# Expert stages: the gate-times-up product traced ahead of the scattered sums and unpinned, low parts of the rows on VectorE, the routing weights' copies behind the first gather

## The chip, the cores and the metric

The kernel runs on one core of one Trainium2 chip. The metric is device time in microseconds (us) of one launch. Before the change it is 1609.78 us, the median of three runs (1607.67 to 1613.72).

## The reference, cut to what matters

Two transformer blocks of two layers each run one after the other on 256 tokens of width 1024, in float32. The change touches only the mixture of experts of the first block, which is run once in each of its two layers:

```python
def grouped_moe(h, router_w, router_b, w_gate, w_up, w_down):
    t = h.reshape(B_ * S, D)
    scores = jax.nn.sigmoid((t @ router_w).astype(jnp.float32))
    sel = scores + router_b.astype(jnp.float32)
    ...  # best group of 4 experts, then the top 2 experts inside that group
    combine = jnp.einsum('nk,nke->ne', top_w, jax.nn.one_hot(top_idx, N_EXPERTS))
    for e in range(N_EXPERTS):
        he = jax.nn.silu(t @ w_gate[e]) * (t @ w_up[e])
        y = y + combine[:, e:e + 1] * (he @ w_down[e])
```

There are 16 experts with hidden width 512, so each layer reads 16 x 3 weight matrices of 2 MB, about 100 MB.

## The kernel before, in words

**An expert stage.** `moe(l)` first finds out which token goes to which expert and then runs eight pairs of experts, p = 0 to 7, two experts side by side on the two halves of TensorE's columns. The head, up to the first pair, goes like this. The 256 rows, as two halves t = 0 and 1, are normalised to `xn` (line 515, VectorE) and copied to DRAM as `xd` (line 1280, a DMA of GpSimd's queue). `parts(t)` splits the rows into a high part `xh` (a copy on ScalarE, line 1272) and a low part `xl`, which is the row less its high part (a subtraction on GpSimd, line 1273), both in an order of columns that reads every fourth element of `xn`. TensorE makes the router's logits, `scored` and a sigmoid make the scores `sc` (lines 1264 and 1288). A chain of small VectorE instructions from `sel` (line 1291) to `pick` (line 1317) chooses the experts; `rk` is a token's place within its expert, `cnt` and `cnti` (lines 1333 to 1338) are the numbers of tokens of the busiest expert of each pair, and `cs` (line 1346) are the routing weights, which `split` copies into a high part `ch` (ScalarE, line 203) and a low part `cl` (VectorE, line 204).

**The first gather.** For pair 0, `hot` builds one-hot tables `kept` on VectorE (line 1359), `gather` multiplies `xh` and `xl` with them on TensorE (line 1373, sixteen products for each half of the width) and ScalarE brings the results to `hg` (line 1377), the moving rows of the gate and up products. The tile of `hg` takes the place of `xn`, so its first write waits until `xn` has been read by the low parts and by the copy to DRAM. `tokens_of` builds further one-hot tables `ohb` on VectorE (line 1391, twelve instructions) from which the token numbers of the later pairs are made; those pairs fetch their rows with indirect DMAs.

**One pair.** `up(p)` runs the gate products `pg` and the up products `pu` (line 1479, 32 matrix instructions each in the trace), then calls `self.pending(2)`, then makes `hd` = silu(gate) on ScalarE (line 1489) and `hd` times up on VectorE (line 1490), then turns `hd` on TensorE (`turn_hidden`, line 184, tile `hT`), calls `self.pending(2)` again, turns the next pair's rows (`hgT`), and `down(p)` runs the down products `po` (line 1527). `self.pending` is the tail of the pair before: its four scattered sums, each two products on TensorE (`py`, lines 1514 and 1515) and an addition into `x` on VectorE (line 1517). Pairs 5 and 6 have a skipped block `rest` (branch at line 1614) between the up products and the sums.

**What sets the order.** The program is written through a planner: it places each engine's instructions by when they are ready in its own model and by program order. `keep_in_program_order`, here `pin`, holds an instruction behind the one that was traced just before it on its engine. So the pinned product of line 1490 stands behind the two additions of line 1517 of the first `pending(2)`. Numbers that branches need (`cnti`) are read into registers by `values_load` (lines 1612 and 1665); the planner has put these reads on TensorE's queue between the first gather and the first gate product. Weights are loaded by SyncE's queue (line 222) into 17 slots of 1 MB; a pair takes 12, and a slot's next load waits until the products that read it are done.

Of the kernel before, what the change touches and what calls it, by code (L numbers as in the profile page):

```python
# [11 lines left out]
F32 = mybir.dt.float32  # L12
# [3 lines left out]
AF = mybir.ActivationFunctionType  # L16
ALU = mybir.AluOpType
# [4 lines left out]
P = 128  # L22
# [98 lines left out]
class Net:  # L121
# [1107 lines left out]
    def moe(self, l):  # L1229
        nc, I, tc = self.nc, self.I, self.tc  # L1230
        V = nc.vector
        mm = nc.tensor.matmul
        A, B = self.scale_shift(l, 1)
        with self.phase(f"moe{l}", MOE_RING, True) as mp:
# [3 lines left out]
            pin = tc.keep_in_program_order  # L1238
# [24 lines left out]
                mm(pl, lg[t], self.fold, start=True, stop=True)  # L1263
                V.scalar_tensor_tensor(sc[:, t, :], pl, rs[t], rb, op0=ALU.mult, op1=ALU.add)

            def parts(t):
                for c in range(2):
                    sl = (slice(None), t, slice(512 * c, 512 * c + 512))

                    hi, lo = (e[sl].rearrange("p (k q) -> p k q", k=4) for e in (xh, xl))  # L1270
                    src = xn[sl].rearrange("p (q k) -> p k q", k=4)
                    pin(nc.scalar.copy(hi, src))
                    pin(nc.gpsimd.tensor_tensor(lo, src, hi.bitcast(F32), op=ALU.subtract))

            xd = self.dram.tile([S, D + NE], F32, name="xd")
            for t in range(2):
# [1 line left out]
                    self.norm_cols(self.norm_turn(self.x, t, k0), hT, t, k0)  # L1278
                rs[t] = self.norm_rows(self.x, t, xn, t)
                pin(nc.gpsimd.dma_start(xd[128 * t:128 * t + 128, 0:D], xn[:, t, :]))  # L1280
            parts(0)
            for t in range(2):
                logits(t)
                self.warm(WARM[t])
# [1 line left out]
                scored(t)  # L1286
            self.warm(WARM[2])
            nc.scalar.activation(sc, sc, AF.Sigmoid)
            parts(1)
            sel = mp.tile([P, 2, 16], F32, name="sel")  # L1290
            V.tensor_tensor(sel, sc, rbias.unsqueeze(1).to_broadcast([P, 2, 16]), op=ALU.add)

# [48 lines left out]
            cs = mp.tile([P, 2, 16], F32, name="cs")  # L1341
# [4 lines left out]
            V.tensor_tensor(cs, cs, den.unsqueeze(2).to_broadcast([P, 2, 16]), op=ALU.mult)  # L1346
            ch = mp.tile([P, 2, 16], F32R, name="ch")
            cl = mp.tile([P, 2, 16], F32R, name="cl")
            self.split(cs, ch, cl)
            nc.gpsimd.dma_start(xd[:, D:].rearrange("(t p) e -> p t e", p=P), cs)  # L1350

            def hot(ps, c0, n):

                m, ohs = 2 * len(ps), []
                io = slots[:, c0:c0 + n].unsqueeze(1).to_broadcast([P, m, n])
                for t in range(2):
                    oh = kept[:, t, :].rearrange("p (e s) -> p e s", e=m)
                    e = rk[:, t, 2 * ps[0]:2 * ps[0] + m].unsqueeze(2).to_broadcast([P, m, n])
                    V.tensor_tensor(oh, e, io, op=ALU.is_equal)
                    ohs.append(oh.rearrange("p e s -> p (e s)"))  # L1360
                return ohs
# [3 lines left out]
            def gather(k0, k1):  # L1365

                if not hg:
                    hg.append(self.sp.tile([P, 2, KD, P], F32, tag="xn", name="hg", bufs=1))
                for b0 in range(k0, k1, 2):
                    ph = self.bank([P, 2, 256], name="ph")  # L1370
                    for b in range(2):
                        for i, (t, xx) in enumerate(((0, xh), (0, xl), (1, xh), (1, xl))):
                            pin(mm(ph[:, b, :], xx[:, t, 128 * (b0 + b):128 * (b0 + b) + 128], oneh[t],
                                   start=i == 0, stop=i == 3))
                    for b in range(2):
                        k = b0 + b
                        nc.scalar.activation(hg[0][:, :, k, :], ph[:, b, :].rearrange("p (a c) -> p a c", a=2), AF.Identity,
                                             scale=self.ab[:, 0, k // 4, k % 4:k % 4 + 1],
                                             bias=self.ab[:, 1, k // 4, k % 4:k % 4 + 1])
# [5 lines left out]
            def tokens_of():  # L1385
                for h in range(2):
                    for t in range(2):
                        o = self.sp.tile([P, 3, 256], BF16, tag=("e2", "gt")[h], name="ohb")
                        e = rk[:, t, 4 + 6 * h:10 + 6 * h].rearrange("p (q j) -> p q j", j=2).unsqueeze(3)
                        for c, n, s0 in ((0, 64, 0), (128, 32, 64), (192, 32, 64)):  # L1390
                            V.tensor_tensor(o[:, :, c:c + 2 * n].rearrange("p q (j s) -> p q j s", j=2),
                                            e.to_broadcast([P, 3, 2, n]),
                                            slots[:, s0:s0 + n].unsqueeze(1).unsqueeze(1).to_broadcast([P, 3, 2, n]),
                                            op=ALU.is_equal)
                        ones_of.append(o)

            def indices():
                px = self.bank([P, 14], name="px")
                for p in range(2, 8):
                    h, q = (p - 2) // 3, (p - 2) % 3  # L1400
                    for c, col in ((0, p), (128, 6 + p)):
                        for t in range(2):
                            mm(px[:, col:col + 1], ones_of[2 * h + t][:, q, c:c + 128], self.tok[:, t:t + 1],
                               start=t == 0, stop=t == 1)

                none = mp.tile([P, 14], F32, name="none")
                V.tensor_copy(number[:, 2:], px[:, 2:])
                V.tensor_scalar(none[:, 2:], number[:, 2:], 0.5, 2.0 * S, op0=ALU.is_lt, op1=ALU.mult)
                V.scalar_tensor_tensor(idx[:, 2:], number[:, 2:], -1.0, none[:, 2:], op0=ALU.add, op1=ALU.add)
                for n in ("xh", "xl"):  # L1410
                    got.append(mp.tile([P, 2, D + NE], F32, tag=n, name=n))
                    V.memset(got[-1][:, :, D:], 0.0)
                rows(0, 2)
                rows(0, 3)
                rows(1, 2)

            def rows(i, p):

                nc.gpsimd.indirect_dma_start(got[i][:, p % 2, :], None, xd[:, :],
                                             bass.IndirectOffsetOnAxis(ap=idx[:, 6 * i + p:6 * i + p + 1], axis=0),  # L1420
                                             bounds_check=S - 1, oob_is_err=False)
# [43 lines left out]
            def up(p, W, between=None):  # L1465

                if p == 0:
                    oneh.extend(hot((0, 1), 0, 64))
                    gather(0, 4)
                    tokens_of()  # L1470
                q = slice(128 * (p % 2), 128 * (p % 2) + 128)
                pg = self.bank([P, 512], name="pg")
                pu = self.bank([P, 512], name="pu")
                for w, pp in ((W[0], pg), (W[1], pu)):
                    for k in range(KD):
                        if p == 0 and w is W[0] and k == 4:
                            gather(4, 8)
                        for j in range(2):
                            pin(mm(pp[64 * j:64 * j + 64, :], hg[0][:, p % 2, k, 64 * j:64 * j + 64], w[j][k // 4][:, k % 4, :],  # L1479
                                   start=k == 0, stop=k == KD - 1, tile_position=(0, 64 * j)))  # L1480
                if between:
                    between()
                if p == 0:
                    indices()

                if self.pending:
                    self.pending(2)
                hd = self.sp.tile([P, 512], F32, tag="e1", name="hd")
                pin(nc.scalar.activation(hd, pg, AF.Silu))
                pin(V.tensor_tensor(hd, hd, pu, op=ALU.mult))  # L1490
                hidT = self.sp.tile([P, 4, P], F32, tag="e2", name="hidT")
                turn_hidden(hd, hidT)
                if self.pending:
                    self.pending(2)
                Sm, ws = places([oneh[t][:, q] for t in range(2)], p) if p < FIRST else own_places.pop(0)
                if 1 <= p < 7:
                    columns(got[0][:, (p + 1) % 2, 0:D], P, hg[0][:, (p + 1) % 2])
                    own_places.append(known(p + 1, 0, kept[:, p % 2, :]))
                    if p < 6:
                        rows(1, p + 2)  # L1500
                    if p < 5:
                        rows(0, p + 3)
                return hidT, Sm, ws

            def turn_hidden(hd, out, bank=None):
                pt = bank.rearrange("p (k n) -> p k n", k=4) if bank is not None else self.bank([P, 4, P], name="hT")
                src = hd.rearrange("p (b q k) -> p b k q", b=2, k=2)
                for k in range(4):
                    self.tr(pt[:, k, :], src[:, k // 2, k % 2, :])
                V.tensor_copy(out, pt)  # L1510
# [951 lines left out]
```

## Time and profile before

| | |
|---|---|
| median of the runs | 1609.78 us (1607.67 to 1613.72) |
| the profiled execution: its time / its span | 1617.59 us / 1615.8 us |
| mean granted TensorE clock | 0.973 of full |
| busy share of the span: TensorE, VectorE, ScalarE, GpSimd | 92%, 57%, 42%, 9% |
| expert stage of layer 0, first gate product to last down product | 226.6 to 469.7 us |
| expert stage of layer 1, likewise | 640.9 to 865.5 us |
| HBM traffic | 422 MB read, 263 GB/s over the span |

All times in the rows are microseconds from the span's start unless marked ns. PE is TensorE's products, PEld its weight loads, DVE VectorE, ACT ScalarE, POOL GpSimd, SP SyncE; a "q" behind a name is the engine's sequencer. A timeline row gives the start, the duration (of all of a merged run, with its count), and in brackets the idle time of the engine before it with what ended it.

### The profile page before, as it was taken

How to read it: one execution, taken by the hardware profiler on the slowest of the kernel's cores; microseconds unless marked ns; L12 is line 12 of the kernel's file. 1: busy time of each engine (PE TensorE's matmuls, PEld its weight loads, DVE VectorE, ACT ScalarE, POOL GpSimd, SP SyncE). 2: the span in 40 equal slices, each digit the busy share in tenths (PEclk: the TensorE clock that was granted, in tenths of full speed). 3: DMA queues.
4: the chain of work that ended last, by engine and by line, in shares of the span. 5: the costliest groups of instructions: out<-in, count | busy, mean ns of one | idle time of the engine just before them, and what ended most of it. 6: DMA issues, size and time to landing. Idle time of an engine off the chain costs nothing. (4 is left out here: it accounts for less than half of the span.)

```text
span 1615.8 us, 22948 instructions
## 1 busy us (share of the span) xinstructions
PE 1494.5 (92%) x8719; PEld 1055.0 (65%) x8719; DVE 920.7 (57%) x1780; ACT 673.9 (42%) x1404; POOL 152.6 (9%) x200
## 2 busy tenths in 40 slices
PE   6999979888989996999888899999999999999998
PEld 3666633333349974443435787878888897788886
DVE  3765533232349985132325776766666776866665
ACT  3434421111135553111114355665555756665554
POOL 0320111000000002110001100110000211110000
PEclk9999989999989998999999899999999999999999
DMA  9988979989948886999997533465564443555640
GB/s 358 335 313 292 368 284 420 418 365 418 405 160 271 276 332 267 400 419 418 417 418 240 175 96 105 151 198 172 182 209 150 155 144 104 169 171 184 207 156 27
DMA packets 172511, 418.14 MB, mean 259 GB/s; under 512 B 10376, under 2 KB 94016, under 8 KB 147792
## 3 DMA queue, kind: packets, MB, share of 16 engines
q1 hardware_dynamic: 165696, 403.46, 67.5%
q0 software_dynamic: 6400, 12.78, 2.4%
q8 instruction: 89, 1.46, 0.4%
q14 instruction: 54, 0.44, 0.1%
q10 hardware_dynamic: 272, 0.00, 0.0%
HBM read 422.13 MB, written 3.19 MB: 263 GB/s over the span
## 5 line engine op out<-in xcount | busy, mean ns | idle before, releaser
L230 DVE TENSOR_TENSOR hl<-w,hl 128x1024 fp32r<-128x1024 f32 x280 | 336.3, 1233 | 56.8 <-ACT hl L229 56.7
L229 ACT CAST hl<-w 128x1024 fp32r<-128x1024 f32 x280 | 280.3, 1045 | 32.6 <-DMA w<-in_even_w_in 11.9
L2337 PE MATMUL pgu<-hT,hl 128*128 128x512 f32 x640 | 224.4, 392 | 0.0
L2338 PE MATMUL pgu<-hT,hl 128*128 128x256 f32 x640 | 178.9, 280 | 0.0
L381 PE MATMUL lin<-hl,hThi 128*128 128x256 f32 (+2 forms) x480 | 158.8, 334 | 1.1 <-ACT hThi L552 0.6
L382 PE MATMUL lin<-hl,hThi 128*128 128x256 f32 (+2 forms) x480 | 152.9, 319 | 3.2 <-DVE hl L230 3.1
L383 PE MATMUL lin<-hl,hTlo 128*128 128x256 f32 (+2 forms) x480 | 152.4, 319 | 0.0
L1517 DVE TENSOR_TENSOR x<-x,py 128x512 f32<-128x512 f32 x68 | 44.0, 683 | 188.2 <-PE py L1515 188.2
L2337 PEld LDWEIGHTS pgu<-hT,hl 128*128 128x128 f32 x640 | 119.8, 187 | 26.5
L1479 PE MATMUL pg<-w,hg 128*64 128x512 f32 x512 | 117.4, 610 | 15.8 <-issue 12.3
L2338 PEld LDWEIGHTS pgu<-hT,hl 128*128 128x128 f32 x640 | 120.8, 189 | 2.0
L1479 PE MATMUL pu<-w,hg 128*64 128x512 f32 x512 | 116.6, 599 | 3.6 <-PEq L1614 3.6
L1527 PE MATMUL po<-w,hidT 128*64 128x512 f32 x512 | 115.3, 603 | 3.8 <-PEq L1670 2.1
L381 PEld LDWEIGHTS lin<-hl,hThi 128*128 128x128 f32 x480 | 92.3, 192 | 17.1 <-issue 8.1
L382 PEld LDWEIGHTS lin<-hl,hThi 128*128 128x128 f32 x480 | 92.2, 192 | 12.5 <-DVE hl L230 5.0
L1479 PEld LDWEIGHTS pg<-w,hg 128*64 128x64 f32 x512 | 41.2, 140 | 88.1 <-issue 73.0
L383 PEld LDWEIGHTS lin<-hl,hTlo 128*128 128x128 f32 x480 | 91.8, 191 | 7.2 <-issue 1.7
L1479 PEld LDWEIGHTS pu<-w,hg 128*64 128x64 f32 x512 | 42.5, 138 | 74.3 <-issue 72.7
L1527 PEld LDWEIGHTS po<-w,hidT 128*64 128x64 f32 x512 | 40.2, 139 | 69.1 <-issue 61.5
L1542 ACT CAST eo<-of 128x512 fp32r<-128x512 f32 x32 | 19.8, 618 | 136.3 <-DVE of L1539 136.1
L1436 ACT ACTIVATE hg<-hgT,ab 128x128 f32<-128x128 f32 x48 | 18.0, 456 | 122.5 <-PE hgT L184 122.4
L381 PE MATMUL linc<-hThi,hl 128*128 128x256 f32 x224 | 66.9, 299 | 0.2 <-ACT hl L229 0.2
(571 smaller groups left out, 2862.2 us busy)
## 6 DMA issues: line engine op xcount, KB each, us to landing
w<-in_exp_w_gate SPq DMA_DIRECT2D x64, 1024.0 KB, 12.0
w<-in_exp_w_down SPq DMA_DIRECT2D x64, 1024.0 KB, 18.2
w<-in_exp_w_up SPq DMA_DIRECT2D x64, 1024.0 KB, 16.1
w<-in_ada_w SPq DMA_DIRECT2D x48, 1024.0 KB, 9.8
w<-in_ffn_wg SPq DMA_DIRECT2D x22, 1024.0 KB, 5.5
w<-in_ffn_wu SPq DMA_DIRECT2D x22, 1024.0 KB, 7.4
w<-in_ffn_wd SPq DMA_DIRECT2D x22, 1024.0 KB, 8.8
w<-in_even_w_in SPq DMA_DIRECT2D x14, 1024.0 KB, 5.1
```

The lines of the kernel that those rows point to most:

```text
L229: pin(self.nc.scalar.copy(w[:, 0], src))
L230: pin(self.nc.vector.tensor_tensor(w[:, 1], src, w[:, 0].bitcast(F32), op=ALU.subtract))
L381: pin(mm(out, lh, rh, start=start, stop=False))
L382: pin(mm(out, lh, rl, start=False, stop=False))
L383: pin(mm(out, ll, rh, start=False, stop=stop))
L1436: nc.scalar.activation(out[:, k, :], pt[:, k, :], AF.Identity, scale=self.ab[:, 0, b, k:k + 1], bias=self.ab[:, 1, b, k:k + 1])
L1479: pin(mm(pp[64 * j:64 * j + 64, :], hg[0][:, p % 2, k, 64 * j:64 * j + 64], w[j][k // 4][:, k % 4, :], start=k == 0, stop=k == KD - 1, til ...
L1517: V.tensor_tensor(xs, xs, py, op=ALU.add)
L1527: pin(mm(po[c][64 * j:64 * j + 64, :], hidT[:, k, 64 * j:64 * j + 64], W[2][j][k // 2][:, k % 2, 512 * c:512 * c + 512], start=k == 0, sto ...
L1542: nc.scalar.copy(eh[c], of)
L2337: mm(pp[i], wh[:, k, :], both[:, :, k, :], start=k == 0, stop=False)
L2338: mm(pp[i][:, 0, :], wl[:, k, :], hi[:, k, :], start=False, stop=k == KD - 1)
```

## The change

Four edits, all in `moe`. `parts` gets a second argument: the ScalarE copies and the low parts are traced in separate calls, and the low parts are VectorE subtractions, pinned; those of t = 0 follow the ScalarE copies directly, those of t = 1 stand in `up(0)` behind `hot` and ahead of `gather(0, 4)`. The copies of the routing weights `ch` and `cl` move from the head to `up(0)`, behind the up products. The silu and the product with up are traced ahead of the first `pending(2)` and are no longer pinned.

```diff
-            def parts(t):
+            def parts(t, low):
...
                     src = xn[sl].rearrange("p (q k) -> p k q", k=4)
-                    pin(nc.scalar.copy(hi, src))
-                    pin(nc.gpsimd.tensor_tensor(lo, src, hi.bitcast(F32), op=ALU.subtract))
+                    if low:
+                        pin(V.tensor_tensor(lo, src, hi.bitcast(F32), op=ALU.subtract))
+                    else:
+                        pin(nc.scalar.copy(hi, src))
...
-            parts(0)
+            parts(0, False)
+            parts(0, True)
...
-            parts(1)
+            parts(1, False)
...
             cl = mp.tile([P, 2, 16], F32R, name="cl")
-            self.split(cs, ch, cl)
...
                 if p == 0:
                     oneh.extend(hot((0, 1), 0, 64))
+                    parts(1, True)
                     gather(0, 4)
                     tokens_of()
...
                 if between:
                     between()
                 if p == 0:
+                    self.split(cs, ch, cl)
                     indices()
+                hd = self.sp.tile([P, 512], F32, tag="e1", name="hd")
+                nc.scalar.activation(hd, pg, AF.Silu)
+                V.tensor_tensor(hd, hd, pu, op=ALU.mult)
 
                 if self.pending:
                     self.pending(2)
-                hd = self.sp.tile([P, 512], F32, tag="e1", name="hd")
-                pin(nc.scalar.activation(hd, pg, AF.Silu))
-                pin(V.tensor_tensor(hd, hd, pu, op=ALU.mult))
                 hidT = self.sp.tile([P, 4, P], F32, tag="e2", name="hidT")
                 turn_hidden(hd, hidT)
```

## Rows read from the trace of the kernel before

**Rows 1.** The page, part 1: busy us, share of the span, instructions

```profile
PE 1494.5 (92%) x8719; PEld 1055.0 (65%) x8719; DVE 920.7 (57%) x1780; ACT 673.9 (42%) x1404; POOL 152.6 (9%) x200
```

**Rows 2.** Waits, whole span: who waited for whom, us in total, times, longest

```profile
PE hT L184 <- DVE hd L1490: 22.4, 16, 1.6
```

**Rows 3.** Timeline of TensorE, layer 0, pair 1, around the end of up

```profile
261.15 7.04 PE L1479 MATMUL pu<-w,hg 128*64 128x512 f32 x32
268.12 0.50 PE L1514 MATMUL py<-eo,kept 128*128 128x512 f32 x1
...
270.92 0.72 PE L184 MATMUL hT<-kt,hd 128*128 128x128 f32 x4 [1.60 <-DVE hd L1490]
```

**Rows 4.** Timeline of VectorE, the same stretch

```profile
268.88 1.28 DVE L1517 TENSOR_TENSOR x<-x,py 128x512 f32<-128x512 f32 x2 [11.85 <-PE py L1515]
270.09 0.68 DVE L1490 TENSOR_TENSOR hd<-hd,pu 128x512 f32<-128x512 f32 x1
```

**Rows 5.** Timeline of VectorE, head of layer 0

```profile
206.74 0.46 DVE L1264 SCALAR_TENSOR_TENSOR sc<-rlT,rstd,rb 128x16 f32<-128x16 f32 x2 [1.02 <-PE rlT L1263]
207.50 5.13 DVE L1291 TENSOR_TENSOR sel<-sc,rbias 128x32 f32<-128x32 f32 x1 [0.30 <-ACT sc L1288]
...
215.65 0.74 DVE L1359 TENSOR_TENSOR kept<-rk,kt 128x256 fp32r<-128x256 f32 x2
...
216.46 3.55 DVE L1391 TENSOR_TENSOR ohb<-rk,kt 128x384 bf16<-128x384 f32 x10
...
220.64 0.15 DVE L1338 CAST cnti<-cnt 1x8 int32<-1x8 f32 x1
```

**Rows 6.** Timeline of VectorE, head of layer 1

```profile
621.91 5.12 DVE L1291 TENSOR_TENSOR sel<-sc,rbias 128x32 f32<-128x32 f32 x1 [0.30 <-ACT sc L1288]
```

**Rows 7.** Timeline of GpSimd, head of layer 0

```profile
206.62 5.96 POOL L1273 TENSOR_TENSOR xl<-xn,xh 128x512 fp32r<-128x512 f32 x4
```

**Rows 8.** One line's view: register reads on TensorE's queue, ns min/median/max, first to last

```profile
L1665 PEldq TENSOR_LOAD <-cnti x12: 295/299/490, 220.8 to 640.1; - x12
...
L1612 PEldq TENSOR_LOAD <-cnti x4: 303/306/308, 223.8 to 639.4; - x4
```

**Rows 9.** Timeline of TensorE, layer 0, the first gate products

```profile
226.63 5.77 PE L1479 MATMUL pg<-w,hg 128*64 128x512 f32 x16 [5.97 <-issue]
```

**Rows 10.** Windows of layer 1: busy by engine, then granted clock, DMA share, GB/s

```profile
640.00:646.00 6.00, 5.13 (x17) 1.65 (x17) 0.00 (x0) 0.00 (x0) 0.00 (x0) 0.67 0.00 0
648.00:846.00 198.00, 180.50 (x854) 77.64 (x854) 53.94 (x89) 27.87 (x68) 13.42 (x13) 0.98 1.01 417
```

**Rows 11.** Landing of pair 7's last up load: layer 0 (issued 420.8), layer 1 (824.7)

```profile
DMA to landing us min/median/max: 15.0/15.0/15.0
...
DMA to landing us min/median/max: 19.8/19.8/19.8
```

**Rows 12.** Timeline of TensorE's weight loads: first products that read those two loads

```profile
453.39 0.17 PEld L1479 LDWEIGHTS pu<-w,hg 128*64 128x64 f32 x2 [0.26 <-issue]
...
849.14 0.17 PEld L1479 LDWEIGHTS pu<-w,hg 128*64 128x64 f32 x2 [0.26 <-issue]
```

**Rows 13.** One line's view: 512 elements, contiguous on VectorE and ScalarE, strided on ScalarE

```profile
L1543 DVE TENSOR_TENSOR eo<-of,eo x32: 651/693/693, 254.3 to 868.1; 128x512 fp32r<-128x512 f32 x32
...
L1542 ACT CAST eo<-of x32: 617/618/619, 253.7 to 866.7; 128x512 fp32r<-128x512 f32 x32
...
L1272 ACT CAST xh<-xn x8: 1105/1118/1133, 201.7 to 622.8; 128x512 fp32r<-128x512 f32 x8
```

**Rows 14.** One line's view, layer 0: copies of xn to DRAM, issued 200.0 and 206.0

```profile
DMA to landing us min/median/max: 8.1/8.5/9.0
```

**Rows 15.** One line's view: the skipped block's branch, and who waited (us, times)

```profile
L1614 PEldq COMPARE_BRANCH x4: 5882/5998/6133, 393.2 to 814.8; - x4
...
  PE pu L1479: 3.6, 2
  PE py L1514: 3.5, 2
```

## The prediction

> **What bounds the kernel now.** The page comes first: TensorE is busy for 92% of the span and no other engine is near it [rows 1], so an edit is worth what it takes from TensorE's idle time, or from the weights it waits for. The waits view then says where TensorE sits idle in the expert stages: 22.4 us in 16 waits before the turning of `hd`, each ended by VectorE's product [rows 2]. The timelines show why. Pair 1's up products end at 268.19 [rows 3]. TensorE runs two scattered sums; VectorE, idle for 11.85 us until then, takes the two additions first (268.88, 1.28 us) and only then the product at 270.09, whose inputs were there since 268.2 [rows 3, 4]. The turning starts at 270.92 after 1.60 us of nothing [rows 3].
>
> The second place is the head. `sel` adds 32 numbers per row and takes 5.13 us [rows 5], and 5.12 us in layer 1 [rows 6]. GpSimd's four low parts run from 206.62 to 212.58 [rows 7]; `sel` ends 0.05 us later. So it is the low parts that hold it, and all behind it waits: `kept`, the gather, and by way of `cnti` at 220.79 the register reads on TensorE's queue [rows 5, 8]. These are eight per layer (six of one line and two of the other); the first starts at 220.8, and the first gate product comes at 226.63, after 5.97 us without a product [rows 8, 9].
>
> Third, the weights. In layer 1 the DMA engines stand still until the first gate products free slots (640 to 646: share 0.00), and are then full, 417 GB/s over the next 198 us [rows 10]. The last up load of pair 7, issued at 824.7, lands at 844.5 and is first read at 849.1: 4.6 us of slack. In layer 0 the same load lands at 435.8 and is read at 453.4: 17.6 us [rows 11, 12].
>
> **The change part by part.** *Product ahead of the sums.* Nothing is added; one instruction per pair moves ahead of two. Unpinned and traced first, the product can start when up ends. It takes 0.68 us, and from its end (270.77) to the turning (270.92) there are 0.15 us [rows 3, 4]; with as much ahead of it the turning is ready 1.0 us after up's end. TensorE meanwhile has the sums' products, from 268.12 until its idle time began, 270.92 less 1.60, or 1.13 us after up's end [rows 3]. So the whole wait goes. Fourteen of the sixteen waits are of this kind (pairs 1 to 7, two layers); pair 0 has no sums, and since fourteen of the longest, 1.6 us, already make 22.4, its two are short. I count 22.0 us: 11.0 in each layer. The additions come 0.7 us later. Behind them on VectorE's queue is the copy of the turned `hd`; product, two additions (1.28 us) and a copy of 0.7 us end at about +2.9 us, when TensorE still has two sums and the next pair's rows to turn. So that costs nothing.
>
> *Low parts on VectorE.* `sel` loses 5.13 less the 0.15 us of a small instruction (`cnti`'s cast), so 5.0 us [rows 5]. In exchange VectorE has four subtractions per layer that the trace has only on GpSimd, at 1.49 us each (5.96 for four) [rows 7]. Bounds for one: 0.69 us, a contiguous VectorE subtraction of this size [rows 13], and 1.49 us. The row closest to the pattern is ScalarE's copy of the same strided rows, 1.118 us against 0.618 contiguous [rows 13]: 0.50 us more for 512 elements, which on top of 0.69 makes 1.2 us, and I take that. [...]
>
> The t = 0 pair is pinned behind `xn` (VectorE's idle time after it begins at 205.7) and stands ahead of `scored`. VectorE is idle for 1.02 us there [rows 5], so of 2.4 us about 1.4 delays `sel` (0.4 to 2.0 by the bounds). The t = 1 pair comes behind `kept`, 2.4 us (1.4 to 3.0). Only the first of it holds the gather, but both stand ahead of `cnti`, if `cnti` keeps its place behind ten of the twelve `ohb` [rows 5]. So the register reads start 5.0 - 1.4 - 2.4 = 1.2 us earlier per layer; by the bounds 3.2 or 0. If the planner now lets `cnti` pass the `ohb` (3.55 us), the gather's end is next, and it is up to 4.9. I take 2.0 us, nearer to the order that the trace has. GpSimd's queue keeps only its DMAs. The second one's place, behind `xn` at 206.0, stays, and it lands 8.1 us on, at 214.1 [rows 14]; `hg` may not be written before, nor before the last low part, some 215. Register reads until about 224 (226.6 less 2) cover that; without that cover it would be what sets the first product.
>
> [...]
>
> *Weights' copies.* `ch` and `cl` are one small instruction each. ScalarE no longer has `ch`, which waits for `cs`, ahead of `hg`. That would start `hg` earlier, but the register reads end later, so nothing is gained. In their new place the 7 us of up products [rows 3] hide them. If that cover were gone they would cost 0.3 us. Zero.
>
> *Sum.* Layer 0: 11.0 + 2.0 = 13.0 us; its slack of 17.6 us covers the faster use of the weights. Layer 1 is different: from the restart on, the loads come at the DMA's rate, and only the restart moves, by the head's 2.0 us. On top TensorE can use up the 4.6 us of slack, and the last wait, 1.6 us, lies behind that load. 2.0 + 4.6 + 1.6 = 8.2 us rather than 13.0. Together 21.2 us. The profiled execution would go from 1617.6 to 1596.4; from the median, 1609.8, the forecast is 1588.6. Its own range is 1581 to 1595: the head at 0 to 4.9 us per layer (17 to 27 us in all), and 2 us of doubt on the slack.
>
> **The rivals.** *The register reads move* (0.20). If `hg` is ready sooner in the planner's account than `cnti`, the first gate products go ahead of the reads. They would start at about 216 (the last low part at 215.2 and one activation), 10.6 us earlier, and the 5.7 us of reads come later on TensorE's queue: a head gain of 4.9, and the DMA's restart 10.6 earlier, so that layer 1 is no longer held by it. 2 x 15.9 = 31.8 us: 1578. For it: `hg` loses `ch`; against: `xn`'s copy to DRAM holds `hg`, too.
>
> *The DMA gives nothing more* (0.10). A queue that is full with twenty microseconds from issue to landing [rows 11] may have no slack to give: layer 1 then gets the head alone, 2 us, 15 in all: 1595.
>
> *The product does not pass the sums* (0.06). If VectorE's order stays, the head's 4 us remain: 1606.
>
> *Slower: the branch comes out from under the up products* (0.04). The branch over `rest` takes 5.9 to 6.1 us on TensorE's queue, 24 us for four [rows 15], of which 7.1 us show as waits of TensorE today, the rest being covered by products already queued. With silu and product now traced right behind that block, the planner may put the branch after the last up product. Then 16.9 us more are bare. After an idle time like the head's the clock is granted at 0.67 of full, the lower of its two levels for much of the stretch [rows 10], and 16 products took 5.77 us [rows 9] where 32 take 7.04 [rows 3], so 2.25 us each, 9 for four. 25.9 - 21.2 is 4.7 us slower than before: 1614.5. It decides from the point where less than 0.5 us of products is queued when the branch starts. Against it: nothing in the diff touches the block.
>
> **How the numbers follow.** The forecast has 0.60. Faster than 1601.7, which is 0.5% and about what a measurement of this kernel can tell from no change: forecast, moved reads and DMA case, 0.60 + 0.20 + 0.09. The product that stays and most of the branch case lie within 0.5%: 0.08. The branch case with a bad head: 0.03 beyond. The range takes in the forecast's own, the moved reads and the DMA case: 1575 to 1598.
>
> **What the profile will show.** Right: the wait of `hT` for `hd` falls from 22.4 us below 2; the product stands ahead of the additions; `sel` takes under 0.3 us; GpSimd has no subtraction of line 1273 and four on VectorE at 1.2 us; the first gate product starts about 2 us earlier after the head's start; waits of TensorE for loads appear in pairs 5 to 7 of layer 1, some 5 us in all, and none in layer 0. Wrong: `sel` still long, so that it waited for something else; the first gate product ahead of the register reads; layer 1 gaining as much as layer 0, so that the DMA did not hold it; or a gap before the scattered sums in the pairs with a branch.

## The result, and the profile after

The changed kernel takes 1590.82 us (median of four runs, 1589.33 to 1593.49) beside 1611.75 for the kernel before (1607.67 to 1614.92): ratio 0.9873, 95% interval 0.9844 to 0.9903, or 20.9 us less, between 16 and 25. The forecast was 1588.6, a gain of 21.2. The sum came out right; its terms did less so, and that their errors cancelled is in part luck.

The page's first part after the change (as in [rows 1]), and the waits of TensorE in layer 1, from 640 to 842 us (us in total, times, longest):

```profile
PE 1481.6 (93%) x8719; PEld 1043.2 (66%) x8719; DVE 916.3 (58%) x1788; ACT 673.7 (42%) x1404; POOL 141.3 (9%) x192
```

```profile
PE py L1518 <- PEq L1618: 5.3, 2, 2.7
PE pu L1482 <- DMA w<-in_exp_w_up: 4.9, 4, 1.3
PE py L1518 <- issue: 2.8, 1, 2.8
...
PE hT L184 <- DVE hd L1491: 0.2, 1, 0.2
```

The wait of [rows 2] is gone but for 0.2 us of pair 0 in each layer. In its place three others stand in layer 1: the loads, the branch of the skipped block (line 1618 now), and a stop that waits for nothing the profile shows ("issue"). Of these the branch was there before, with 4.2 us (line 1614); the loads cost 0.3 us then, and the stop was not there:

```profile
PE pu L1479 <- PEq L1614: 2.5, 1, 2.5
PE py L1514 <- PEq L1614: 1.7, 1, 1.7
```

The same stretch as in [rows 3, 4], TensorE first, then VectorE:

```profile
257.00 7.04 PE L1482 MATMUL pu<-w,hg 128*64 128x512 f32 x32
263.97 0.50 PE L1518 MATMUL py<-eo,kept 128*128 128x512 f32 x1
...
265.00 0.68 PE L184 MATMUL hT<-kt,hd 128*128 128x128 f32 x4
```

```profile
264.19 0.69 DVE L1491 TENSOR_TENSOR hd<-hd,pu 128x512 f32<-128x512 f32 x1 [11.30 <-PE pu L1482]
264.79 1.28 DVE L1521 TENSOR_TENSOR x<-x,py 128x512 f32<-128x512 f32 x2
265.99 0.68 DVE L1514 COPY hidT<-hT 128x512 f32<-128x512 f32 x1
```

The product now ends the idle time of VectorE, the additions follow, and the turning starts 1.03 us after the first sum instead of 2.80. The head of layer 0 on VectorE (as [rows 5]), TensorE (as [rows 9]) and ScalarE:

```profile
203.81 2.04 DVE L1273 TENSOR_TENSOR xl<-xn,xh 128x512 fp32r<-128x512 f32 x2
205.77 0.36 DVE L1264 SCALAR_TENSOR_TENSOR sc<-rlT,rstd,rb 128x16 f32<-128x16 f32 x2
206.42 0.19 DVE L1294 TENSOR_TENSOR sel<-sc,rbias 128x32 f32<-128x32 f32 x1 [0.29 <-ACT sc L1291]
...
210.44 2.01 DVE L1273 TENSOR_TENSOR xl<-xn,xh 128x512 fp32r<-128x512 f32 x2
...
216.57 0.15 DVE L1341 CAST cnti<-cnt 1x8 int32<-1x8 f32 x1
```

```profile
222.55 5.72 PE L1482 MATMUL pg<-w,hg 128*64 128x512 f32 x16 [9.23 <-issue]
```

```profile
215.40 0.22 ACT L203 CAST ch<-cs 128x32 fp32r<-128x32 f32 x1 [6.99 <-DVE cs L1349]
215.54 1.93 ACT L1379 ACTIVATE hg<-ph,ab 128x256 f32<-128x256 f32 x4
```

`sel` takes 0.19 us instead of 5.13, the four subtractions cost VectorE 4.05 us, and `ch` still stands ahead of `hg` on ScalarE. TensorE still has its register reads between `cnti` and the first gate product (six of the eight per layer, as in [rows 8], with the first and last start in us at the end):

```profile
L1669 PEldq TENSOR_LOAD <-cnti x12: 294/299/487, 216.8 to 619.6; - x12
```

To see where the time went I use three stretches of each trace: a layer from the router's last small product (`rlT`, line 1263) to the end of its last down product, and the rest of the program from there. Before: 469.73 - 206.31 = 263.4 us in layer 0, 865.49 - 620.73 = 244.8 in layer 1, 1615.8 - 865.5 = 750.3 behind it. The other rows are worked out the same way. The stretches are those of one profiled execution each; the times are medians, for e6 to e9 of a single execution. The runs come from several chips.

| kernel | layer 0 | layer 1 | behind | time |
|---|---|---|---|---|
| before | 263.4 | 244.8 | 750.3 | 1611 to 1616, by chip |
| after | 246.5 | 239.3 | 745.8 | 1590.8 |
| e5: pins off alone | 251.0 | 239.1 | 745.0 | 1594.1 |
| e2: low parts alone | 258.7 | 242.4 | 749.8 | 1607.0 |
| e6: after, half the low parts on GpSimd | 248.7 | 238.2 | 745.8 | 1590.4 |
| e7: before, fewer loads in layer 1 | 264.2 | 237.3 | 748.0 | 1608.3 |
| e8: after, fewer loads in layer 1 | 247.3 | 226.0 | 744.9 | 1576.6 |
| e12: pins off in layer 0 | 250.5 | 244.2 | 749.9 | 1601.3 |
| e13: pins off in layer 1 | 262.8 | 242.0 | 748.5 | 1609.7 |
| e10: reads in pair 1 | 240.5 | 229.1 | 746.0 | 1574.8 |
| e11: e10 and `ch` behind `hg` | 235.6 | 229.3 | 749.6 | 1570.3 |
| e9: after, `ch` behind `hg` | 247.9 | 240.5 | 747.2 | 1593.5 |
| e15: e11, block in the middle of up | 233.8 | 229.4 | 745.7 | 1566.2 |
| e14: before, idle time filled | 262.5 | 243.7 | 748.1 | 1613.9 |

So layer 0 gave 16.9 us, layer 1 5.5, and the stages behind, which the diff doesn't touch, 4.5. That is 26.9, more than the medians' 20.9: the profiled execution of before, 1617.6, lies 6 us above its median, that of after 1.5 below. So differences of a us or less between two rows of the table say nothing.

### The profile page after: what moved, and what is told of

It is laid out like the page before. It is cut to its first block, busy times and chain, and to the rows that moved or that the text cites. A ratio compares the mean times of both kernels' runs of the same rounds, so it can differ in the third digit from the quotient of the medians.

```text
span 1587.5 us, 22950 instructions
## 1 busy us (share of the span) xinstructions
PE 1481.6 (93%) x8719; PEld 1043.2 (66%) x8719; DVE 916.3 (58%) x1788; ACT 673.7 (42%) x1404; POOL 141.3 (9%) x192
## 5 line engine op out<-in xcount | busy, mean ns | idle before, releaser
L229 ACT CAST hl<-w 128x1024 fp32r<-128x1024 f32 x280 | 280.2, 1045 | 33.5 <-DMA w<-in_even_w_in 20.5
L1491 DVE TENSOR_TENSOR hd<-hd,pu 128x512 f32<-128x512 f32 x16 | 11.0, 688 | 196.9 <-PE pu L1482 196.9
```

Of the source, the lines that this page charges most:

```text
L229: pin(self.nc.scalar.copy(w[:, 0], src))
```

## The experiments

**What the edits are, once built.** Three things are seen in the built order alone. The kernel before with only the two pins taken off, nothing moved, has the same instructions in the same order on every engine as the one with the two lines moved and unpinned. The changed kernel with both pinned at their new place is again the changed kernel. And with `split` left in its old place it is still the changed kernel, instruction for instruction. So what counts in the first edit is that the product isn't pinned *behind the sums*, and the third edit does nothing at all: tracing `ch` later doesn't move it in ScalarE's queue.

**e5_unpinned: pins off alone.**

```diff
-                pin(nc.scalar.activation(hd, pg, AF.Silu))
-                pin(V.tensor_tensor(hd, hd, pu, op=ALU.mult))
+                nc.scalar.activation(hd, pg, AF.Silu)
+                V.tensor_tensor(hd, hd, pu, op=ALU.mult)
```

> The kernel before with one edit: the silu and the product of gate and up are no longer pinned; they stay where they were traced, behind the scattered sums. Built, this gives the same order of instructions on every engine as tracing them ahead of the sums. Low parts stay on GpSimd. Theory (the wait of TensorE for the product goes in both layers, but in layer 1 the DMA engines give back only the slack that the weights had): layer 0 from the first gate product to the end 14 us shorter (seven waits of 1.75 us and some 2 us of clock), layer 1 5.5 us shorter (4.6 of slack and the wait behind the last load), 19.5 us in all, about 1591. sel still takes 5.1 us. Rival (layer 1 loses its gain in the changed kernel to something of the head or of the copies, not to the DMA): layer 1 14 us shorter too, 28 us in all, about 1583. Rival (the pin was not what held the product): no change, 1610.

1594.06 us beside 1611.3, ratio 0.9897 (0.9870 to 0.9923). Layer 0 gave 12.4 us, layer 1 5.6, the stages behind 5.3. Layer 0 was expected to give 14. Layer 1 gave less than half of layer 0, without any change to the head. What layer 1 loses has to do with the layer, not with the other edits.

**e2_low: low parts alone.**

```diff
-                    pin(nc.scalar.copy(hi, src))
-                    pin(nc.gpsimd.tensor_tensor(lo, src, hi.bitcast(F32), op=ALU.subtract))
+                    if low:
+                        pin(V.tensor_tensor(lo, src, hi.bitcast(F32), op=ALU.subtract))
+                    else:
+                        pin(nc.scalar.copy(hi, src))
...
                     oneh.extend(hot((0, 1), 0, 64))
+                    parts(1, True)
                     gather(0, 4)
```

> The kernel before with the low parts alone moved from GpSimd to VectorE (t = 0 behind its ScalarE copies, t = 1 behind kept). Theory (GpSimd's subtractions held sel, and of the 5 us that this frees the VectorE subtractions and the register reads leave half): sel 0.2 us, a subtraction about 1.0 us on VectorE, the first gate product 2.5 us earlier in layer 0 and a further 2.2 in layer 1, the stages behind it unchanged in length: 4.7 us in all, about 1606. Rival (sel waited for something else): sel still 5 us, and the VectorE subtractions make the head longer: 1612 or more. Rival (the whole of what sel lost comes back): 10 us, 1600.

1606.98 beside 1611.3, ratio 0.9966 (0.9946 to 0.9985), 4.3 us between the medians. `sel` takes 0.19 us; from `rlT` to the first gate product it is 18.13 us instead of 20.32, and 17.96 instead of 20.14 in layer 1: 2.2 us each.

**e6_half_low: how `sel` was held.** The changed kernel with the subtractions of t = 0 back on GpSimd.

```diff
-                        pin(V.tensor_tensor(lo, src, hi.bitcast(F32), op=ALU.subtract))
+                        pin((V, nc.gpsimd)[1 - t].tensor_tensor(lo, src, hi.bitcast(F32), op=ALU.subtract))
```

> The changed kernel, but the low parts of t = 0 stay on GpSimd, as in the kernel before; those of t = 1 are on VectorE. It tells how sel was held. Theory (sel is held until the last of the subtractions queued on GpSimd is done): two of them instead of four, 3.0 us, so sel takes 2.1 us and ends within 0.1 us of the second one's end. Rival (sel waits only for the one that runs when it starts): sel 1.0 us or less and ends with the first one. In the first case cnti and the first gate product come about 1.6 us later per layer than in the changed kernel (2.0 us more sel, 0.4 us of VectorE's work that had delayed it gone): 1592 to 1594; in the second some 0.5 us: 1591.

GpSimd and VectorE in the head of layer 0:

```profile
206.45 3.02 POOL L1273 TENSOR_TENSOR xl<-xn,xh 128x512 fp32r<-128x512 f32 x2
```

```profile
207.33 2.20 DVE L1294 TENSOR_TENSOR sel<-sc,rbias 128x32 f32<-128x32 f32 x1 [0.30 <-ACT sc L1291]
```

GpSimd ends at 209.47, `sel` at 209.53: it is held until the last subtraction queued there is done, also when there are two. The first gate product comes 1.3 us later than in the changed kernel (19.33 us from `rlT`, not 18.06), 1.6 were expected; the one time, 1590.4, doesn't show it.

**e7_light_before and e8_light_after: the loads of layer 1.** Before and after, each without 24 MB of layer 1's up weights (the up products of pairs 2 to 7 read the gate weights in their place), run once:

```diff
-                return [weights("exp_w_gate", 512, p), weights("exp_w_up", 512, p)]
+                g = weights("exp_w_gate", 512, p)
+                return [g, g if l and p > 1 else weights("exp_w_up", 512, p)]
```

> The kernel before, but in layer 1 the up products of pairs 2 to 7 read the gate weights, and those up weights are not loaded (24 MB of layer 1's weights left out); the amount of TensorE's work is the same. It is the partner of the changed kernel with the same cut. Theory (in the kernel before the DMA just keeps up in layer 1): layer 1 as long as in the kernel before, within 2 us; the loads now land 15 us or more ahead of their use.

> The changed kernel with the same cut: in layer 1 the up products of pairs 2 to 7 read the gate weights, and those up weights are not loaded. Theory (in layer 1 the DMA engines take back what the removed waits give): with the cut no product of layer 1 waits for a load, the branches of the skipped block are covered as in the kernel before, and layer 1, from the first gate product to its end, is 13 to 15 us shorter than in the kernel before with the same cut, as layer 0 is; in all 30 us between the two. Rival (layer 1 lost its gain to the branches or to the clock, whatever the loads do): layer 1 only 4 to 6 us shorter, 21 us in all.

Between the two there are 31.6 us (1608.26 and 1576.64) where the full kernels differ by 20.9. Layer 1 becomes 11.3 us shorter instead of 5.5 (237.3 to 226.0), and no product waits for a load. TensorE's waits in layer 1 of e8:

```profile
PE py L1519 <- issue: 2.3, 1, 2.3
...
PE py L1518 <- PEq L1619: 0.6, 2, 0.3
```

The branch costs 0.6 us there and 5.3 in the changed kernel. So the loads hold back a good part of layer 1's gain, by their own 4.9 us of waits and by way of the branch. Two expectations failed. From the first gate product to the end, layer 1 of e8 is 9.1 us shorter than that of e7 (217.1 and 208.0), not 13 to 15, and the stop is left with 2.3. And e7 itself was to leave layer 1 of the kernel before as it was, and took 7.5 us from it, 1.5 and 3.3 of them up to the first sums of pairs 5 and 6, the pairs with a branch. The branch's waits fell there from 4.2 to 1.2 us. Its rows are 5.9 to 6.2 us in the kernels before and after, and in layer 1 3.7 us in three of the four in e7 and e8: fewer loads go with a shorter branch, but why is not shown, so e7 and e8 change two things at once.

**e12_layer0 and e13_layer1: pins off in one layer.**

```diff
+                own = pin if l else (lambda i: i)       # e13: pin if not l
-                pin(nc.scalar.activation(hd, pg, AF.Silu))
-                pin(V.tensor_tensor(hd, hd, pu, op=ALU.mult))
+                own(nc.scalar.activation(hd, pg, AF.Silu))
+                own(V.tensor_tensor(hd, hd, pu, op=ALU.mult))
```

> The kernel before with the pins off in layer 0 alone; layer 1 keeps them. In the built order two things follow from that in layer 1: all 16 instructions of pair 6's up products stand ahead of the skipped block rest, where the kernel before has 11 ahead and 5 behind, and the stage behind layer 1 keeps the order that it has in the kernel before. Theory: layer 0 with its head 12 to 13 us shorter; in layer 1 the block's new place alone costs 2 to 4 us (the wait of 2.85 us between pair 6's scattered sums, which the changed kernel has and the kernel before has not, and the lower clock behind it); the stage behind layer 1 as before, 748 to 750 us from the last down product to the end: 9 to 11 us less in all, 1600 to 1602 beside 1611. Rival (the wait between pair 6's sums belongs to the unpinned product or to the late weights): layer 1 as in the kernel before, 1598.

> The kernel before with the pins off in layer 1 alone. In the built order pair 6's up products of layer 1 stay split 11 and 5 around the skipped block, and the stage behind layer 1 keeps the order of the kernel before. Theory (what layer 1 gives is bounded by the weights' landing, and the wait between pair 6's sums, with the clock behind it, took another 2 to 4 us of it): layer 1 with its head 8 us shorter, where pins off in both layers gave 5.6; no wait between pair 6's sums; the stage behind it 748 to 750 us, not 745: 8 us less in all, about 1603 beside 1611. Rival (the weights alone set layer 1): 5.6 us. Rival (the stage behind layer 1 is faster because layer 1 ends otherwise, not for its order): it takes 745 us here too, and 1599.

e12: 1601.28 beside 1613.35, ratio 0.9936 (0.9912 to 0.9959); layer 0 gave 12.9 us. In its layer 1, whose product is still pinned, the stop between pair 6's sums appears all the same; it belongs to the block's place:

```profile
807.79 0.47 PE L1515 MATMUL py<-eo,kept 128*128 128x512 f32 x1 [2.40 <-PEq L1615]
...
813.34 0.59 PE L1515 MATMUL py<-eo,kept 128*128 128x512 f32 x1 [1.74 <-issue]
```

But layer 1 is 0.6 us shorter, not 2 to 4 longer: as far as one trace tells, the block costs about the same with the stop as without. e13 shows it from the other side: 1609.73, ratio 0.9977 (0.9961 to 0.9993), layer 1 only 2.8 us shorter. The stop is gone, and the branch, now between the up products, is bare for 5.21 us:

```profile
812.97 1.08 PE L1479 MATMUL pu<-w,hg 128*64 128x512 f32 x4 [1.30 <-DMA w<-in_exp_w_up]
819.26 5.24 PE L1479 MATMUL pu<-w,hg 128*64 128x512 f32 x10 [5.21 <-PEq L1615]
```

The row ahead of it goes with that: the last four products before the branch, 1.08 us of work, had waited 1.30 us for their load, so that little was left to cover the branch. My expectation of 8 us took the stop for the loss; it was the smaller form of it.

**The stages behind layer 1.** In the changed kernel, e5, e6, e8 to e11 and e15 the planner puts the first instructions behind layer 1 in another order than before; in e2, e7, e12, e13 and e14 in the old one. The old order takes 748.0 to 750.3 us in six traces, the new one 744.9 to 747.2 in seven of eight. VectorE and TensorE, before:

```profile
889.74 0.74 DVE L619 TENSOR_SCALAR R<-lin,rs 128x512 f32<-128x512 f32 x1
890.40 1.22 DVE L230 TENSOR_TENSOR hl<-w,hl 128x1024 fp32r<-128x1024 f32 x1
```

```profile
891.67 0.50 PE L382 MATMUL lin<-hl,hThi 128*128 128x512 f32 x1 [2.25 <-DVE hl L230]
```

and after:

```profile
864.28 1.22 DVE L230 TENSOR_TENSOR hl<-w,hl 128x1024 fp32r<-128x1024 f32 x1
865.42 0.74 DVE L619 TENSOR_SCALAR R<-lin,rs 128x512 f32<-128x512 f32 x1
```

```profile
865.56 0.50 PE L382 MATMUL lin<-hl,hThi 128*128 128x512 f32 x1 [0.83 <-DVE hl L230]
```

A weight's low part (line 230) now stands ahead of `R`, and TensorE waits 0.83 instead of 2.25 us. That is 1.4 of some 3 us; the rest is not traced. e13 ends layer 1 with the product unpinned and keeps the old order and 748.5: the order goes with the time, not the way in which layer 1 ends. A second place farther on (lines 1995 to 2005 in the kernel before) is in another order, too, with a wait of TensorE of 0.9 us before and none after; there e12 and e13 have the changed kernel's order, e8 nearly the old one, and their times, 749.9, 748.5 and 744.9, go with the first place all the same. In the exception, e11 with 749.6, ScalarE waits 2.4 us longer there for the load of `mem`. No run changes this order alone; that it is the cause is likely, not shown.

**e14_filled: idle time and clock.** The kernel before with useless products in the idle time.

```diff
                     self.pending(2)
+                    self.warm(5)
                 hd = self.sp.tile([P, 512], F32, tag="e1", name="hd")
```

> The kernel before with five useless bfloat16 products of 512 columns on TensorE behind the first two scattered sums of each pair, in the place where it waits 1.6 us for the product of silu and up. The order of the rest stays. It takes TensorE's idle time away and leaves the wait. Theory (after some of the fourteen idle times the clock falls to half for the products behind them; 5 of 14 in the trace of before, at 1.0 to 1.5 us each): none of the fourteen is followed by half clock, the sums behind each turning start 0.23 us apart, and the time falls by 3 to 7 us, 1604 to 1608 beside 1611. Rival (the idle time is not what lets the clock fall): still some of the fourteen at 0.43 us, and 1611, or more if the useless products delay the turning.

In the kernel before 5 of the 14 waits are followed by a lower clock; two stretches from a turning to the down products, the first with it, the second without (the last three numbers are the granted clock as a share of full, the DMA share and GB/s):

```profile
459.30:462.20 2.90, 2.66 (x8) 1.76 (x8) 1.56 (x3) 0.00 (x0) 0.00 (x0) 0.56 1.10 347
298.20:301.00 2.80, 2.60 (x16) 2.27 (x16) 2.02 (x4) 0.62 (x2) 0.00 (x0) 1.00 1.01 421
```

In e14 the waits are down to 0.4 or 0.5 us and it is 1 of 14, but the time is 1613.86 beside 1613.35 (ratio 1.0008, 0.9995 to 1.0021): nothing, on balance. The branch is bare for 5.8 us in layer 1 there instead of 4.2, which may hide a small gain. The traces of e2 and e7, with the waits, have 3 and 2. So these falls differ from run to run, and filling the idle time gains nothing beyond the spread; 3 to 7 us was too much. They may be a part of the 6 us by which the profiled execution of before was long; that is not shown.

**e9, e10, e11: what the head waits for now.** e9 pins `ch` behind the gather, e10 moves the register reads, e11 does both.

```diff
-                    self.split(cs, ch, cl)                          # e9, e11
+                    pin(nc.scalar.copy(ch, cs))
+                    V.tensor_tensor(cl, cs, ch.bitcast(F32), op=ALU.subtract)
...
+                        if p == 1 and k % 2:                        # e10, e11
+                            with self.tc.issue_after(i.ins):        # i: the product just traced
+                                read()                              # the next of the eight values_load
```

> The changed kernel with the copy ch pinned on ScalarE, where the change only traced it later: ch now really stands behind the eight hg activations of the first gather. Theory (the register reads on TensorE's queue end later than hg): hg starts about 2.5 us earlier (213 instead of 215.5 in the changed kernel's trace), the register reads and the first gate product stay where they are, the time stays within 2 us of 1590.8. Rival (hg sets the first product): the first gate product 2.5 us earlier in each layer, 1586.

> The changed kernel with the eight register reads of each layer on TensorE's queue moved from ahead of the first gate product to between the products of pair 1, one behind every four matrix instructions of gate and up. Theory (the reads are what the first product waits for, and one read of 0.7 us at a time hides under queued products): the first gate product starts with hg, 5 us earlier in each layer, the DMA engines restart as much earlier in layer 1, pair 1's gate and up products take no longer than 14.5 us as now: 10 us in all, up to 13 if the clock does not fall in the shorter idle time: 1577 to 1581. Rival (the reads stop TensorE wherever they stand): pair 1 takes 5 us longer, 1590. Rival (in layer 1 the DMA takes it back): 5 us, 1586.

> Both of the two above: the reads between pair 1's products, and ch behind the first gather on ScalarE. Theory: without the reads hg sets the first product, so that now ch counts: the first gate product another 2.5 us earlier in each layer than with the reads moved alone, 5 us in all, up to 9 if the clock stays up: 1570 to 1576. Rival (hg is then held by something else, the copy of xn to DRAM or the low parts): less than 1 us in each layer against the reads moved alone.

e9: `hg` starts 8.4 us behind `rlT` instead of 11.1, released by the copy of `xn` to DRAM as the prediction had it, and the first gate product stays at 18.06; the one time is 1593.48. So the reads count, not `hg`:

```profile
214.53 1.93 ACT L1379 ACTIVATE hg<-ph,ab 128x256 f32<-128x256 f32 x4 [4.48 <-DMA xd<-xn]
```

e10: 1574.76 us. ScalarE's `hg` ends TensorE's wait now, and the eight reads are hidden in pair 1, whose 64 instructions take 14 us as before:

```profile
217.27 5.35 PE L1482 MATMUL pg<-w,hg 128*64 128x512 f32 x16 [2.83 <-ACT hg L1379]
...
244.50 7.04 PE L1482 MATMUL pg<-w,hg 128*64 128x512 f32 x32
251.36 7.04 PE L1482 MATMUL pu<-w,hg 128*64 128x512 f32 x32
```

From `rlT` to the first gate product it is 11.70 us instead of 18.06. Layer 1 gave 10.2 us against 6.0 in layer 0; 2.8 us of that are its first sixteen products, which ran at full clock (3.65 us, not 6.46). The windows over these sixteen in layer 1, of the changed kernel and of e10 (0.55 against 1.00 of full):

```profile
620.40:626.80 6.40, 6.39 (x16) 1.92 (x16) 0.00 (x0) 0.00 (x0) 0.00 (x0) 0.55 0.00 0
```

```profile
609.10:612.70 3.60, 3.52 (x16) 1.06 (x16) 0.73 (x5) 1.39 (x4) 0.34 (x1) 1.00 0.31 127
```

e11: 1570.30 us. Now `ch` counts: layer 0 gave another 4.9 us, layer 1 nothing, where 2.5 each were expected; its first product came 1.6 us earlier, and then its waits for loads are 4.8 us instead of e10's 3.6 and the stop in pair 6 3.5 instead of 2.0.

**e15_branch: the block in the middle of up.** e11 and

```diff
+                        if between and w is W[1] and k == 4:
+                            between()
```

> The kernel with the reads between pair 1's products and ch behind the gather, and in it the skipped block traced in the middle of the up products of pairs 5 and 6 (10 instructions ahead of the branch and 6 behind it, in both layers) instead of behind them. Theory (the second stop, of 2 to 4 us between pair 6's scattered sums in layer 1, comes with the block's place right ahead of the sums): it is gone, the stops at the branch itself stay at 1 to 2.7 us: 2 to 4 us less than without it, 1566 to 1569 beside 1570.3. Rival (the stop comes with the number of instructions since the branch and only moves): the same time, with a stop of 2 us or more between later products of pair 6 in layer 1.

1566.17 us (1564.4 to 1567.27), against before 0.9712 (0.9694 to 0.9730); e11 has 0.9723 (0.9684 to 0.9762), so the two are not told apart. The mechanism isn't what I expected: the stop between pair 6's sums is gone, and the branch is bare for 9.5 us in two waits instead (5.4 in e11); layer 1 takes 229.4 us beside 229.3 in e11.

```profile
PE pu L1482 <- PEq L1631: 9.5, 2, 5.1
```
e15 has the lowest median here, 24.7 us below the changed one, 20.5 of it from the reads and `ch`.

## Why the prediction was right, point by point

- **The product passes the sums: right.** 11.0 us per layer were counted, seven waits of 1.6; in layer 0 each turning gained 1.7 to 1.8, 12.1 in all, and the layer gave 12.4 in e5, where the head is as before. Low by about 1 us. The further 2.2 us that layer 0 gave in this pair of traces (16.9 less 12.4 and the head's 2.3) have no one cause here: 0.9 of it is that the first sixteen products took 6.66 us in e5 and 5.72 in the changed kernel.
- **`sel` and the low parts: right.** 0.19 us, not 0.15; a subtraction 1.06 us in the line's median where I took 1.2, between the bounds 0.69 and 1.49: strided 1.06, contiguous 0.69 [rows 13]. In e6, too, `sel` waited for both of the queued subtractions (it ended at 209.53, they at 209.47), not for the running one alone.
- **The head: the number right, partly by luck.** 2.0 us were forecast, 2.3 and 2.2 came (20.32 to 18.06, 20.14 to 17.96). But the prediction's sum for the order that stayed was 1.2; 2.0 leaned towards `cnti` passing the `ohb`, and it did not. It stands behind all twelve of them, before as after: behind the ten of [rows 5] there were two more.

```profile
220.10 0.61 DVE L1391 TENSOR_TENSOR ohb<-rk,kt 128x192 bf16<-128x192 f32 x2
```

What made up for it is that the subtractions cost less than forecast: `sel` starts 0.74 us later behind `rlT`, not 1.4 (1.93 and 1.19), and the pair of t = 1 takes 2.0 us, not 2.4: 4.94 - 0.74 - 2.0 = 2.2. The reads kept their place ahead of the first product, as [rows 8, 9] had it; e10 proves their price.
- **The copies: zero, for another reason.** I wrote that ScalarE no longer has `ch` ahead of `hg`. It has; the edit changes nothing in the built kernel.
- **Layer 1: the mechanism right, two terms off.** 4.9 us of waits for loads in pairs 5 and 6 were forecast as "some 5 us in pairs 5 to 7". The term that was too large is the head's 2.0 us in this layer: pins off alone gave 5.6 us there (e5), and with the head 5.5. They did not all reach the DMA: the first sixteen products took 6.46 us instead of 5.17, at a granted clock of 0.55 instead of 0.70, and the first load behind the standstill (after in the line's view, before in the timeline) was issued 24.4 us behind `rlT` (626.9 - 602.45) instead of 25.3 (646.05 - 620.73): 0.9 us earlier, not 2.2.

```profile
L222 SPq DMA_DIRECT2D w<-in_exp_w_up x2: 328/356/385, 626.9 to 627.3; - x2
```

```profile
646.05 0.81 SPq L222 DMA_DIRECT2D w<-in_exp_w_up  x2
```

The other is what late loads cost besides their own waits, as they take the branch's cover: the branch's waits went from 4.2 to 5.3 us, to 7.9 in e13, and the stop of 2.8 came with the block's place. 8.2 were forecast, 5.5 came. The last loads waited for were pair 6's, not pair 7's: pair 7's last up load, issued at 805.8, landed at 825.6 and kept nobody waiting.
- **The stages behind: missed.** I had nothing there; some 3 us (six traces against eight) to 4.5 (this pair) go with the planner's new order.
- **The sum.** 13.0 + 8.2 + 0 = 21.2 forecast; 16.9 + 5.5 + 4.5 = 26.9 in the traces, of which some 6 us are the long execution of before. The step that fixed the forecast, taking the gain worked out in the profiled execution off the median, came out only because the missed terms are about as large as that excess. That the sum met the medians to 0.3 us is luck; the two main waits were named rightly.
- **The rivals.** The reads did not move by themselves; the DMA gave something; the product passed. The branch rival came true in a corner: in layer 1 all of pair 6's up products now stand ahead of the block, as it supposed, and the sign that was named for it, a gap before the sums of the pairs with a branch, is there (2.7 and 2.6 us in pairs 5 and 6). But e12, in one trace, puts the price of that at nothing.

## What to carry to other kernels

A pin behind the instruction traced last orders against everything traced before, and taking it off can be the whole edit; tracing an instruction later moves nothing unless an edge holds it there, so read the built order of each engine before you credit an edit. Ask what runs at its limit in a stage: layer 1, where the DMA engines had a share of 1.01 (415 GB/s, 628 to 824 us of the changed kernel), gave 5.5 us here and 11.3 between e7 and e8, which load 24 MB less. And look at what covers a branch: behind products that came late for their load, 5.21 us of one stood bare in e13. After a re-plan look at stages that the diff doesn't touch, and ask what stands in front of the first product once the old cause is gone: here register reads, worth 16 us (e10).

## What the hardware showed that I had not expected

- A small VectorE addition (`sel`) was held through all queued GpSimd subtractions: 5.13 us for four (before), 2.20 for two (e6), 0.19 for none (after).
- The branch over the skipped block took 5.9 to 6.2 us on TensorE's queue in the kernels before and after, up to 6.5 in e7, but 3.7 in three of four cases with fewer loads (layer 1 of e7 and e8). In the stretch of the changed kernel with the branch and the stop (794 to 802 us, and again 800 to 808), the DMA view shows one packet of the instruction queue beside the weights:

```profile
q1 hardware_dynamic: 458, 3.33, 100.4%
q8 instruction: 1, 0.02, 0.9%
```

Whether that packet has to do with the branch is not shown: the same queue has 89 over the whole span, and single ones in stretches of layer 1 without a branch, too (648 to 652 us, 672 to 676). So no run here shows what the 6 us and the "issue" stop wait for.
- Idle times of 1.5 to 1.6 us were followed by a clock of about half in 5, 3 and 2 of 14 cases of three traces (before, e2, e7), and 7.8 us ahead of the first gate products of layer 1 by a clock of 0.55 of full over all sixteen (the changed kernel, 620.4 to 626.8 us): 0.50 in each half microsecond from 620 to 626 and 1.00 from 626.5 on. The 0.67 of [rows 10] is made up likewise: 0.50 from 641 to 642 us, 1.00 from 644 to 645.
- A register read on TensorE's queue took 0.3 us, and from the first of eight in a row to the first gate product it was 5.8 us, 0.7 for each (216.8 to 222.55 in the changed kernel); with one behind every four matrix instructions pair 1 stayed at 14 us (e10).
